# One K tile first, unread products at the start, parameters mid-way: reordering the first stage of a hybrid layer

## The chip, the cores and the metric

The kernel runs on one core of a Trainium2 chip. The metric is the device time of one execution in microseconds (us); less is better. The chip has five engines with queues of their own: PE (TensorE, matrix products), DVE (VectorE), ACT (ScalarE), POOL (GpSimd) and SP (SyncE, which here only issues DMA transfers). Each engine takes its instructions strictly in the order of its queue; between engines they wait on semaphores.

## The reference, cut to what matters

One layer of a streaming encoder for 256 prompt positions and 32 sample positions, 288 columns in all, in fp32:

```python
xn   = rmsnorm(x, norm_mix_pre)
proj = xn @ w_in                 # -> u_pool | z | xs, B, C | dt
pool = pool_mixer(u_pool, ...)
ssd  = ssd_mixer(z, xBC, dt, ...) # causal conv, chunked scan, gate, norm
x    = x + rmsnorm(concat[pool, ssd] @ w_out, norm_mix_post)
x    = x + rmsnorm(ConvFFN(rmsnorm(x, norm_ffn_pre)), norm_ffn_post)
```

D_MODEL is 2048 (16 K tiles of 128 rows). Only the beginning concerns us: the read of x and the product of xn with the columns of w_in for B (256), C (256) and dt (32).

## The kernel before, in words

Activations lie with features on the partitions and the 288 positions along the free axis. Every fp32 product is made of three products in a faster format: the weight block `raw` is split into a high part `whi` (ACT) and a rest `wlo` (DVE), the activation likewise, and PE adds high x high (L162), high x low (L163) and low x high (L164) into one PSUM bank. `project()` does this for a group of output columns over all K tiles; weights are streamed by SP into four `raw` buffers, and `whi` and `wlo` have four buffers each.

The first stage reads x itself. `input_tiles()` issues the transfers of `xt` (two blocks of 128 prompt rows) and `xs_` (32 sample rows), and for each K tile transposes them on PE (L298, L299, L300) into one bank of three that serve small results. From there ACT writes the high half of `xn`, scaled by the gain g (L119), DVE the low half (L120), and DVE a copy `xT` (L303) that is stored to DRAM for the residual (L305). The gain comes from `g_in`, transposed by `columns()` (L280, L281). The normalisation by the root mean square is applied later: ACT squares whole rows of xt and xs_ (L347, L348), PE spreads the result over the partitions (L354, `prs`), and DVE copies it to `rstd` (L358). Each accumulator of the stage is then multiplied by rstd as it is emptied (`conv_in()`, L379 and L380).

The stage is one call of `project()` with three groups, B, C and dt, which accumulate in five banks (all that the accumulators have). The K tiles go in steps of 2, 2, 4, 4, 4, with the next step's tiles asked for ahead of this step's products. dt is 32 columns wide, so `split_narrow()` puts both halves side by side and needs two products (L184, L185). At K tile 12 `parameters()` transposes the small parameters (`columns()` and L324, copied by L281 and L325). After the stage come the xs columns of w_in, 256 at a time, with the same accumulator banks.

POOL sets constants at the start (ident, ones, tri, rec, scan_one, four `ebuf` by L244), and then issues the transfers of the small parameters. DVE derives `sel`, `pick` and `sel64` from ident (L235 to L238). A scheduler orders each engine's queue by priority; what is marked `keep_in_program_order` stays in the order of the source.

Of the kernel before, what the change touches and what calls it, by code (L numbers as in the profile page):

```python
# [35 lines left out]
HALF = NF // 2  # L36
MW = 416
EVAC = 100
XS_RATE = (0, 0, 1, 0, 1, 0, 1, 0)
Z_RATE = (1, 0, 1, 1, 0, 1, 1, 0)  # L40
TAIL = NT - P
# [3 lines left out]
def body(  # L45
# [78 lines left out]

    ahead = [0]

    def fetch_w(view, kb, nk, c0, nc_):
        raw = wpool.tile([P, nk, nc_], F32, tag="raw", name="raw")
        with tc.high_priority(offset=ahead[0]):
            sp.dma_start(out=raw, in_=view[:, kb : kb + nk, c0 : c0 + nc_])  # L130
        return raw

    def split_w(raw, kb, nk, nc_, after=()):

        out = []
        step = min(nk, 1024 // nc_)
        for k in range(0, nk, step):
            n = min(step, nk - k)
            hi = wpool.tile([P, n, nc_], F32R, tag="hi", name="whi")
            lo = wpool.tile([P, n, nc_], F32R, tag="lo", name="wlo")  # L140
            with ExitStack() as order:
                order.enter_context(tc.high_priority(offset=ahead[0]))
                for ins in after:
                    order.enter_context(tc.issue_after(ins.ins))
                act.activation(hi, raw[:, k : k + n, :], AF.Copy)  # L145
                dve.tensor_tensor(lo, raw[:, k : k + n, :], hi.bitcast(F32), op=ALU.subtract)  # L146
            out.append([(kb + k + i, hi[:, i, :], lo[:, i, :]) for i in range(n)])
        return out

    def split_narrow(raw, kb, nk, nc_, after):  # L150

        both = xin.tile([P, nk, 2, nc_], F32R, tag="both", bufs=2, name="both")
        with ExitStack() as order:
            order.enter_context(tc.high_priority(offset=ahead[0]))
            for ins in after:
                order.enter_context(tc.issue_after(ins.ins))
            act.activation(both[:, :, 0, :], raw, AF.Copy)
            dve.tensor_tensor(both[:, :, 1, :], raw, both[:, :, 0, :].bitcast(F32), op=ALU.subtract)
        return [(kb + k, both[:, k, :, :].rearrange("p r c -> p (r c)")) for k in range(nk)]

    def mm3(out, wh, wl, a, start, stop):
# [4 lines left out]
    def project(view, groups, acts, ksplit, before=None, done=None, spare=(), hold=(), behind=None):  # L166


        n_all = sum(-(-w // P) for _, w in groups)
        accs = [acc_ps.tile([P, NT], F32, tag="acc", name="acc") for m in range(n_all - len(spare))]  # L170
        accs.extend(spare)
        k_first, k_last = ksplit[0][0], ksplit[-1][0] + ksplit[-1][1] - 1
        after = before(*ksplit[0]) if before else None
        for i, (kb, n) in enumerate(ksplit):
            raws = [fetch_w(view, kb, n, c0, w) for c0, w in groups]
            nxt = None
            if before and i + 1 < len(ksplit):
                nxt = before(*ksplit[i + 1])
            m0 = 0
            for raw, (c0, w) in zip(raws, groups):  # L180
                if w < P:
                    for k, both in split_narrow(raw, kb, n, w, after or ()):
                        o = accs[m0][: 2 * w, :]
                        pe.matmul(o, both, acts[k][:, 0, :], start=k == k_first, stop=False)  # L184
                        pe.matmul(o, both, acts[k][:, 1, :], start=False, stop=k == k_last)  # L185
                    continue
# [12 lines left out]
            after = nxt  # L199
        return accs  # L200

    def blocks_out(d, t, src, pool_):
# [15 lines left out]
    pool.affine_select(  # L218
        out=tri, in_=ones, pattern=[[1, P]], compare_op=ALU.is_ge, fill=0.0, base=0, channel_multiplier=-1
    )  # L220
    eps_t = const.tile([P, 1], F32, name="eps_t")
    pool.memset(eps_t, EPS)
    warm = const.tile([P, 1], F32, name="warm")
    tc.keep_in_program_order(act.activation(warm, eps_t, AF.Copy))
# [7 lines left out]
    sel = const.tile([HEADS, 2], F32, name="sel")  # L232
    pick = const.tile([HEADS, NX], F32, name="pick")
    id32 = ident[:HEADS, :HEADS]
    dve.tensor_reduce(sel, id32.rearrange("h (t r) -> h r t", r=2), axis=AX.X, op=ALU.add)  # L235
    dve.tensor_reduce(pick, id32.rearrange("h (t r) -> h t r", r=2), axis=AX.X, op=ALU.add)
    sel64 = const.tile([HEADS, 2, 64], F32, name="sel64")
    dve.tensor_copy(sel64, sel.unsqueeze(2).broadcast_to([HEADS, 2, 64]))  # L238

    NE = 4  # L240
    ebuf = []
    for i in range(NE):
        e = const.tile([P, 326], F32, name=f"ebuf{i}")
        pool.memset(e, 0.0)  # L244
        ebuf.append(e)

    start = ExitStack()
    xin = start.enter_context(tc.tile_pool(name="xin", bufs=1))

    g0_in = xin.tile([KD, P], F32, name="g0_in")  # L250
    act.dma_start(out=g0_in, in_=rows(norm_mix_pre))
# [3 lines left out]
    pool.dma_start(out=pb_in[76:92, :], in_=rows(norm_ffn_pre))  # L255
    pool.dma_start(out=pb_in[92:108, :], in_=rows(norm_ffn_post))
    xt = xin.tile([P, 2, D_MODEL], F32, name="xt")
    xs_ = xin.tile([NS, D_MODEL], F32, name="xs_")
    xpv = x_prompt.rearrange("o (b p) d -> p (o b) d", p=P)
    pa_in = xin.tile([124, P], F32, name="pa_in")  # L260
    pool.dma_start(out=pa_in[0:80, :], in_=rows3(ssd_conv_w))
# [15 lines left out]
    def columns(src, n, name):  # L277
        o = const.tile([P, n], F32, name=name)
        p_ = aux([P, n], "pt")
        pe.transpose(p_, src, ident[:n, :n])  # L280
        dve.tensor_copy(o, p_)  # L281
        return o

    g_mix_pre = columns(g0_in, KD, "g0")


# [1 line left out]
    xT = xin.tile([P, KD, NT], F32, name="xT")  # L288
    xT_d = dram.tile([P, KD, NT], F32, name="xT_d")

    def input_tiles(kb, n):
        c = slice(kb * P, (kb + n) * P)
        sp.dma_start(out=xt[:, :, c], in_=xpv[:, :, c])
        sp.dma_start(out=xs_[:, c], in_=x_sample[0][:, c])
        for t in range(kb, kb + n):
            p_ = aux([P, NT], "pt")
            c = slice(t * P, (t + 1) * P)
            pe.transpose(p_[:, 0:P], xt[:, 0, c], ident)  # L298
            pe.transpose(p_[:, P:NP_], xt[:, 1, c], ident)  # L299
            pe.transpose(p_[:, NP_:NT], xs_[:, c], ident[:NS, :NS])  # L300
            a = atile("xn")
            last = split_from(a, p_, g_mix_pre[:, t : t + 1])
            dve.tensor_copy(xT[:, t, :], p_)  # L303
            xn.append(a)
        act.dma_start(out=xT_d[:, kb : kb + n, :], in_=xT[:, kb : kb + n, :])  # L305
        return last

    def parameters():
        pb = columns(pb_in, 108, "pb")
# [18 lines left out]
    prm = []  # L328

    def first_in(kb, n):  # L330
        if kb == 12:
            prm.extend(parameters())
        return input_tiles(kb, n)

    win = w_in.rearrange("o (k p) c -> p (o k) c", p=P)
    O_Z, O_X = D_POOL, D_POOL + D_SSD
    O_B, O_C, O_DT = O_X + D_SSD, O_X + D_SSD + 256, O_X + CONV
    first = project(
        win, [(O_B, 256), (O_C, 256), (O_DT, HEADS)], xn, [(0, 2), (2, 2), (4, 4), (8, 4), (12, 4)], first_in
    )  # L340

    ahead[0] = 200
    ssum = xin.tile([P, 3], F32, name="ssum")
    pool.memset(ssum, 1.0)
    junk = xin.tile([P, D_MODEL], F32, name="junk")
    for b in range(2):
        act.activation(junk, xt[:, b, :], AF.Square, accum_out=ssum[:, b : b + 1])  # L347
    act.activation(junk[:NS, :], xs_, AF.Square, accum_out=ssum[:NS, 2:3])  # L348
    rs = xin.tile([P, 3], F32, name="rs")
    act.activation(rs, ssum, AF.Sqrt, bias=eps_t, scale=1.0 / D_MODEL)  # L350
    dve.reciprocal(rs, rs)
    p_ = aux([P, NT], "prs")
    for b, (o, n) in enumerate(BLK):
        pe.matmul(  # L354
            p_[:, o : o + n], rs[:n, b : b + 1].broadcast_to([n, P]), ident[:n, :n], start=True, stop=True
        )
    rstd = const.tile([P, NT], F32, tag="spread", bufs=3, name="rstd")
    dve.tensor_copy(rstd, p_)  # L358

# [784 lines left out]
```

## Time and profile before

| | |
|---|---|
| median of three runs | 1360.85 us (1360.6, 1360.85, 1362.29) |
| the profiled execution | 1361.99 us; span in the trace 1360.2 us |
| mean granted clock of PE | 0.995 |
| PE busy | 1340.6 us, 99% of the span |
| DVE, ACT, POOL busy | 879.0, 666.9, 234.3 us |
| DMA | 252.13 MB, mean 185 GB/s |

Times in a trace count from the start of the span. The span is what the profiler saw of the engines; the execution's own time holds 1.8 us more that lie around it. Busy time of PE counts a matrix product until its modelled end, so neighbouring products overlap, and a stretch in which PE counts as busy may still run at a lower rate: the distance from one start to the next tells that.

### The profile page before, as it was taken

Reading aid. Unit: us, or ns where it says so; the run is one execution under the profiler, and the core shown is the slowest. Engines: PE = TensorE matmul, PEld = TensorE weight load, DVE = VectorE, ACT = ScalarE, POOL = GpSimd, SP = SyncE. Lnnn points to the kernel's source line nnn. Section 1 sums busy time; section 2 is a strip of 40 time slices with the busy share of each in tenths; the row PEclk is TensorE's granted clock in tenths of the full one; section 3 lists DMA queues with packets and bytes.
Section 4 is the critical chain, followed back from the end, with each engine's and each line's share of the span. In section 5 each row is a group of like instructions: output and inputs, shape, how many; then the busy total and the mean of one; then the engine's idle time right before and its main releaser. Section 6 shows DMA issues by size and latency. Waiting matters only on the chain.

```text
span 1360.2 us, 25798 instructions
## 1 busy us (share of the span) xinstructions
PE 1340.6 (99%) x10231; PEld 1330.2 (98%) x10231; DVE 879.0 (65%) x1515; ACT 666.9 (49%) x1000; POOL 234.3 (17%) x394
## 2 busy tenths in 40 slices
PE   8999999999999999999999999999999999999996
PEld 7999999999999999999999999999999999999995
DVE  6898988679544468977666644335666666654443
ACT  6557757446434455654444433334444444454441
POOL 3132112132224310211121100001111111101110
PEclk9999999999999999999999999999999999999998
DMA  9869995465656536766554545554544545577662
GB/s 267 248 188 284 261 261 162 138 215 172 217 183 209 170 109 196 228 185 191 177 164 156 172 148 169 171 178 155 179 162 157 182 158 161 173 224 198 181 174 87
DMA packets 300135, 252.13 MB, mean 185 GB/s; under 512 B 75728, under 2 KB 293050, under 8 KB 299886
## 3 DMA queue, kind: packets, MB, share of 16 engines
q1 hardware_dynamic: 296810, 243.20, 58.6%
q0 software_dynamic: 2320, 4.65, 1.2%
q10 hardware_dynamic: 884, 2.63, 0.5%
q8 instruction: 80, 1.31, 0.4%
q14 instruction: 41, 0.34, 0.1%
HBM read 236.13 MB, written 14.31 MB: 184 GB/s over the span
## 4 chain that ended last, share of the span: by engine, by line
PE 97%; DMA 1%; DVE 1%; ACT 0%; issue 0%; DVEq 0%; ACTq 0%
PE acc L162 31%; PE acc L164 31%; PE acc L163 31%; PE pst L842 1%; PE py L561 1%; DMA raw<-in_w_up 1%; DVE xr L1102 0%; DVE wlo L146 0%; PE py L563 0%; DMA xt<-in_x_prompt 0%; PE pt L298 0%; ACT whi L145 0%; PE pt L300 0%; PE acc_x L162 0%; PE acc_x L163 0%
## 5 line engine op out<-in xcount | busy, mean ns | idle before, releaser
L146 DVE TENSOR_TENSOR wlo<-raw,whi 128x1024 fp32r<-128x1024 f32 (+1 forms) x416 | 494.0, 1189 | 365.2 <-ACT whi L145 359.3
L145 ACT ACTIVATE whi<-raw 128x1024 fp32r<-128x1024 f32 (+1 forms) x416 | 427.2, 1028 | 513.4 <-PE acc L163 436.9
L162 PE MATMUL acc<-hn,whi 128*128 128x288 f32 x1376 | 404.8, 296 | 0.6 <-DVE ebuf L943 0.6
L163 PE MATMUL acc<-hn,whi 128*128 128x288 f32 x1376 | 403.6, 294 | 0.0
L164 PE MATMUL acc<-hn,wlo 128*128 128x288 f32 x1376 | 403.4, 294 | 0.0
L164 PEld LDWEIGHTS acc<-hn,wlo 128*128 128x128 f32 x1376 | 260.0, 189 | 0.0
L163 PEld LDWEIGHTS acc<-hn,whi 128*128 128x128 f32 x1376 | 260.0, 189 | 0.0
L162 PEld LDWEIGHTS acc<-hn,whi 128*128 128x128 f32 x1376 | 257.5, 188 | 0.8 <-PE acc_x L164 0.8
L162 PE MATMUL acc<-xn,whi 128*128 128x288 f32 x704 | 209.5, 299 | 0.0
L162 PE MATMUL acc<-fa,whi 128*128 128x288 f32 x704 | 208.7, 296 | 0.0
L163 PE MATMUL acc<-fa,whi 128*128 128x288 f32 x704 | 208.6, 296 | 0.0
L163 PE MATMUL acc<-xn,whi 128*128 128x288 f32 x704 | 208.3, 297 | 0.0
L164 PE MATMUL acc<-fa,wlo 128*128 128x288 f32 x704 | 208.2, 296 | 0.0
L164 PE MATMUL acc<-xn,wlo 128*128 128x288 f32 x704 | 207.6, 297 | 0.0
L163 PEld LDWEIGHTS acc<-xn,whi 128*128 128x128 f32 x704 | 134.0, 191 | 0.2
L164 PEld LDWEIGHTS acc<-xn,wlo 128*128 128x128 f32 x704 | 133.3, 190 | 0.3
L162 PEld LDWEIGHTS acc<-xn,whi 128*128 128x128 f32 x704 | 132.7, 189 | 0.4
L163 PEld LDWEIGHTS acc<-fa,whi 128*128 128x128 f32 x704 | 133.0, 189 | 0.0
L162 PEld LDWEIGHTS acc<-fa,whi 128*128 128x128 f32 x704 | 132.4, 188 | 0.0
L164 PEld LDWEIGHTS acc<-fa,wlo 128*128 128x128 f32 x704 | 132.2, 188 | 0.0
L944 POOL COPY fc_stage<-ebuf 128x4 f32<-128x4 f32 x88 | 27.0, 307 | 511.8 <-DVE ebuf L943 466.6
L950 DVE SCALAR_TENSOR_TENSOR fc<-ebuf,pf,fc 128x290 f32<-128x290 f32 x176 | 90.1, 516 | 3.0 <-ACT fc L948 0.3
(317 smaller groups left out, 1622.2 us busy)
## 6 DMA issues: line engine op xcount, KB each, us to landing
raw<-in_w_up SPq DMA_DIRECT2D x80, 1024.0 KB, 5.2
raw<-in_w_in SPq DMA_DIRECT2D x40, 1024.0 KB, 5.8
raw<-in_w_down SPq DMA_DIRECT2D x32, 1024.0 KB, 5.3
raw<-in_w_out SPq DMA_DIRECT2D x24, 1024.0 KB, 6.4
raw<-in_w_down SPq DMA_DIRECT2D x16, 768.0 KB, 4.6
raw<-in_w_up SPq DMA_DIRECT2D x14, 512.0 KB, 4.2
gb<-g_d SPq DMA_DIRECT2D x8, 832.0 KB, 4.8
raw<-in_w_in SPq DMA_DIRECT2D x6, 512.0 KB, 6.4
```

The source lines that it names most:

```text
L145: act.activation(hi, raw[:, k : k + n, :], AF.Copy)
L146: dve.tensor_tensor(lo, raw[:, k : k + n, :], hi.bitcast(F32), op=ALU.subtract)
L162: pe.matmul(out, wh, a[:, 0, :], start=start, stop=False)
L163: pe.matmul(out, wh, a[:, 1, :], start=False, stop=False)
L164: pe.matmul(out, wl, a[:, 0, :], start=False, stop=stop)
L561: ins = pe.matmul(y[c, 0:256], xw[:, 0, f_], m[:, h, 0:256], start=True, stop=False)
L842: ins = pe.matmul(st[:, o, :], x_, btok[:, gi, b, :], start=b != 1, stop=b != 0)
L944: pool.tensor_copy(fc_stage[:, :, :, i], e[:, 256:324].rearrange("p (s c) -> p s c", c=34)[:, :, 0:2])
L950: dve.scalar_tensor_tensor(c, e[:, r_ : r_ + 290], pf[:, r_, i : i + 1], c, op0=ALU.mult, op1=ALU.add)
```

## The change

The first stage is written out in place of the call of `project()`:

- K tiles come in steps of 1, 1, 1, 1, 2, 2, 2, 3, 3 (`FIRST`). For each, SP issues the transfer of xt and then one of the weights of B, C and dt together, 544 columns; three steps are issued ahead. The first 256 columns of xs_ come by ACT's queue, the rest by one transfer of SP's, after the second step. xT is stored in three transfers (`STORES`).
- PE runs products that nobody reads (`keep_busy()`): seven ahead of the transpose of g, five after tile 0's transposes. Their operand `busy` is filled by three DVE copies from `ones`.
- For K tile 0, the products high x high and high x low of all four blocks stand ahead of tile 1's transposes, and low x high behind them. From then on a step's products follow the transposes of the next step.
- xs_ is now 128 rows high with zeros in the first 96 (DVE and POOL set them), so that its transpose (L309) is a full product with ident's last 32 columns; the three products that spread rstd (L425) have 128 rows likewise.
- `parameters()` comes with step 6 (`PARAMETERS`), that is K tile 8, and no longer with K tile 12.
- sel, pick and sel64 are made after the stage.

The diff, cut to its core:

```diff
+FIRST = ((0, 1), (1, 1), (2, 1), (3, 1), (4, 2), (6, 2), (8, 2), (10, 3), (13, 3))
+STORES = {3: 0, 9: 4, 15: 10}
+BUSY = (7, 5)
+PARAMETERS = 6
...
+    busy = xin.tile([P, NT], F32R, name="busy")
+    for o, n in BLK:
+        tc.keep_in_program_order(dve.tensor_copy(busy[:, o : o + n], ones[:, 0:n]))
+
+    xs_ = xin.tile([P, D_MODEL], F32, name="xs_")
+    tc.keep_in_program_order(dve.memset(xs_[: P - NS, : 2 * P], 0.0))
...
+    pool.memset(xs_[: P - NS, 2 * P :], 0.0)
     NE = 4
     ebuf = []
...
-    xs_ = xin.tile([NS, D_MODEL], F32, name="xs_")
+    tc.keep_in_program_order(act.dma_start(out=xs_[P - NS :, : 2 * P], in_=x_sample[0][:, : 2 * P]))
+    tc.keep_in_program_order(act.activation(warm, eps_t, AF.Copy))
+    busy_ps = aux([P, NT], "busy_ps")
+
+    def keep_busy(n):
+
+        for _ in range(n):
+            tc.keep_in_program_order(pe.matmul(busy_ps, busy[:, 0:P], busy, start=True, stop=True))
...
+    keep_busy(BUSY[0])
     g_mix_pre = columns(g0_in, KD, "g0")
...
+    def input_tile(t):
+        p_ = aux([P, NT], "pt")
+        c = slice(t * P, (t + 1) * P)
+        pin = tc.keep_in_program_order if t < 4 else lambda ins: ins
+        pin(pe.transpose(p_[:, 0:P], xt[:, 0, c], ident))
+        pin(pe.transpose(p_[:, P:NP_], xt[:, 1, c], ident))
+        pin(pe.matmul(p_[:, NP_:NT], xs_[:, c], ident[:, P - NS :], start=True, stop=True))
...
+        def split():
+            pin(act.activation(a[:, 0, :], p_, AF.Copy, scale=g_mix_pre[:, t : t + 1]))
+            pin(dve.scalar_tensor_tensor(
+                a[:, 1, :], p_, g_mix_pre[:, t : t + 1], a[:, 0, :].bitcast(F32), op0=ALU.mult, op1=ALU.subtract
+            ))
+
+        def keep():
+            pin(dve.tensor_copy(xT[:, t, :], p_))
+            if t in STORES:
+                c = slice(STORES[t], t + 1)
+                act.dma_start(out=xT_d[:, c, :], in_=xT[:, c, :])
...
-    first = project(
-        win, [(O_B, 256), (O_C, 256), (O_DT, HEADS)], xn, [(0, 2), (2, 2), (4, 4), (8, 4), (12, 4)], first_in
-    )
+    first = [acc_ps.tile([P, NT], F32, tag="acc", name="acc") for _ in range(5)]
+    raws = {}
+
+    def first_load(i):
+        if i < len(FIRST):
+            kb, n = FIRST[i]
+            input_load(kb, n)
+            raws[i] = fetch_w(win, kb, n, O_B, NB + HEADS, pin=True)
+
+    for i in range(3):
+        if i == 2:
+            c = slice(2 * P, D_MODEL)
+            tc.keep_in_program_order(sp.dma_start(out=xs_[P - NS :, c], in_=x_sample[0][:, c]))
+        first_load(i)
+    def first_tiles(i):
+        if i == PARAMETERS:
+            prm.extend(parameters())
+        return [input_tile(t) for t in range(FIRST[i][0], sum(FIRST[i]))] if i < len(FIRST) else []
+
+    prm = []
+    steps = first_tiles(0)
+    keep_busy(BUSY[1])
+    for i, (kb, n) in enumerate(FIRST):
+        first_load(i + 3)
+        pin = i < 4
+        ahead_steps = first_tiles(i + 1) if i else []
+        for split, _ in steps:
+            split()
+        raw = raws.pop(i)
+        parts = split_w(raw[:, :, :NB], kb, n, NB, pin=pin)
+        for _, keep in steps:
+            keep()
+        narrow = split_narrow(raw[:, :, NB:], kb, n, HEADS, pin)
+        if not i:
+            (_, hi, lo), = parts.pop()
+            for w, r in ((hi, 0), (hi, 1), (lo, 0)):
+                if w is lo:
+                    ahead_steps = first_tiles(1)
+                for m in range(4):
+                    tc.keep_in_program_order(pe.matmul(
+                        first[m], w[:, m * P : (m + 1) * P], xn[0][:, r, :], start=w is hi and not r, stop=False
+                    ))
+        for part in parts:
+            for m in range(4):
+                c = slice(m * P, (m + 1) * P)
+                for k, hi, lo in part:
+                    mm3(first[m], hi[:, c], lo[:, c], xn[k], k == 0, k == KD - 1)
+        for k, both in narrow:
+            o = first[4][: 2 * HEADS, :]
+            pe.matmul(o, both, xn[k][:, 0, :], start=k == 0, stop=False)
+            pe.matmul(o, both, xn[k][:, 1, :], start=False, stop=k == KD - 1)
+        steps = ahead_steps
 
     ahead[0] = 200
+    sel = const.tile([HEADS, 2], F32, name="sel")
...
+    dve.tensor_copy(sel64, sel.unsqueeze(2).broadcast_to([HEADS, 2, 64]))
...
-        pe.matmul(
-            p_[:, o : o + n], rs[:n, b : b + 1].broadcast_to([n, P]), ident[:n, :n], start=True, stop=True
-        )
+        pe.matmul(p_[:, o : o + n], rs[:, b : b + 1].broadcast_to([P, P]), ident[:, P - n :], start=True, stop=True)
```

In the changed kernel the lines of the same statements have other numbers: the three products of a step are L170, L171 and L172 (for K tile 0 L392), the transposes L307 to L309, xn L314 and L315, xT L320, the splits L152 and L153, the parameter copies L288 and L344, the copies into busy L227, the unread products L264, rstd L427, and the accumulators are emptied by L448 and L449. In DVE's queue the rstd copy is followed by an instruction of the mixer (`hv`, L539), a split of weights (L153) and then L448 and L449.

More of the change, by code (lines that the diff above doesn't have):

```diff
@@ L125, in body, with fetch_w, split_w @@
     ahead = [0]
-    def fetch_w(view, kb, nk, c0, nc_):
+    def fetch_w(view, kb, nk, c0, nc_, pin=False):
         raw = wpool.tile([P, nk, nc_], F32, tag="raw", name="raw")
         with tc.high_priority(offset=ahead[0]):
-            sp.dma_start(out=raw, in_=view[:, kb : kb + nk, c0 : c0 + nc_])
+            ins = sp.dma_start(out=raw, in_=view[:, kb : kb + nk, c0 : c0 + nc_])
+            if pin:
+                tc.keep_in_program_order(ins)
         return raw
-    def split_w(raw, kb, nk, nc_, after=()):
+    def split_w(raw, kb, nk, nc_, after=(), pin=False):
         out = []
@@ L144, in split_w, with split_narrow @@
                     order.enter_context(tc.issue_after(ins.ins))
-                act.activation(hi, raw[:, k : k + n, :], AF.Copy)
-                dve.tensor_tensor(lo, raw[:, k : k + n, :], hi.bitcast(F32), op=ALU.subtract)
+                parts = (
+                    act.activation(hi, raw[:, k : k + n, :], AF.Copy),
+                    dve.tensor_tensor(lo, raw[:, k : k + n, :], hi.bitcast(F32), op=ALU.subtract),
+                )
+                if pin:
+                    for ins in parts:
+                        tc.keep_in_program_order(ins)
             out.append([(kb + k + i, hi[:, i, :], lo[:, i, :]) for i in range(n)])
         return out
-    def split_narrow(raw, kb, nk, nc_, after):
+    def split_narrow(raw, kb, nk, nc_, pin):
+        pin = tc.keep_in_program_order if pin else lambda ins: ins
         both = xin.tile([P, nk, 2, nc_], F32R, tag="both", bufs=2, name="both")
[L153 to L158, printed above, removed]
+        pin(act.activation(both[:, :, 0, :], raw, AF.Copy))
+        pin(dve.tensor_tensor(both[:, :, 1, :], raw, both[:, :, 0, :].bitcast(F32), op=ALU.subtract))
         return [(kb + k, both[:, k, :, :].rearrange("p r c -> p (r c)")) for k in range(nk)]
@@ L180, in project @@
             for raw, (c0, w) in zip(raws, groups):
[L181 to L186, printed above, removed]
                 parts = split_w(raw, kb, n, w, ((after or ()) if m0 else ()) + (hold if i else ()))
@@ L220, in body @@
     )
+    start = ExitStack()
+    xin = start.enter_context(tc.tile_pool(name="xin", bufs=1))
+    busy = xin.tile([P, NT], F32R, name="busy")
[3 more added lines that the diff above has]
+    tc.keep_in_program_order(dve.memset(xs_[: P - NS, : 2 * P], 0.0))
     eps_t = const.tile([P, 1], F32, name="eps_t")
@@ L223, in body @@
     warm = const.tile([P, 1], F32, name="warm")
-    tc.keep_in_program_order(act.activation(warm, eps_t, AF.Copy))
     rec = const.tile([P, 16], F32, name="rec")
@@ L231, in body @@
         pool.memset(scan_one[:, c : c + 1], 0.0)
[L232 to L238, printed above, removed]
+    pool.memset(xs_[: P - NS, 2 * P :], 0.0)
     NE = 4
@@ L245, in body @@
         ebuf.append(e)
-    start = ExitStack()
-    xin = start.enter_context(tc.tile_pool(name="xin", bufs=1))
     g0_in = xin.tile([KD, P], F32, name="g0_in")
@@ L289, in body, with input_load @@
     xT_d = dram.tile([P, KD, NT], F32, name="xT_d")
-    def input_tiles(kb, n):
+    def input_load(kb, n):
         c = slice(kb * P, (kb + n) * P)
[L293 to L306, printed above, removed]
+        tc.keep_in_program_order(sp.dma_start(out=xt[:, :, c], in_=xpv[:, :, c]))
+    def input_tile(t):
[5 more added lines that the diff above has]
+        pin(pe.matmul(p_[:, NP_:NT], xs_[:, c], ident[:, P - NS :], start=True, stop=True))
+        a = atile("xn")
+        xn.append(a)
+        def split():
[8 more added lines that the diff above has]
+                act.dma_start(out=xT_d[:, c, :], in_=xT[:, c, :])
+        return split, keep
     def parameters():
@@ L326, in parameters @@
         return pb, pah, g_mix_post, g_ffn_pre, g_ffn_post, pa, p_scale, g_ssd, pc, pf
[L328 to L333, printed above, removed]
     win = w_in.rearrange("o (k p) c -> p (o k) c", p=P)
     O_Z, O_X = D_POOL, D_POOL + D_SSD
-    O_B, O_C, O_DT = O_X + D_SSD, O_X + D_SSD + 256, O_X + CONV
-    first = project(
-        win, [(O_B, 256), (O_C, 256), (O_DT, HEADS)], xn, [(0, 2), (2, 2), (4, 4), (8, 4), (12, 4)], first_in
-    )
@@ L342, in body @@
-    ahead[0] = 200
+    O_B = O_X + D_SSD
+    NB = 512
+    first = [acc_ps.tile([P, NT], F32, tag="acc", name="acc") for _ in range(5)]
[10 more added lines that the diff above has]
+        first_load(i)
@@ new lines, in body @@
+    ahead[0] = 200
+    sel = const.tile([HEADS, 2], F32, name="sel")
+    pick = const.tile([HEADS, NX], F32, name="pick")
+    id32 = ident[:HEADS, :HEADS]
+    tc.keep_in_program_order(dve.tensor_reduce(sel, id32.rearrange("h (t r) -> h r t", r=2), axis=AX.X, op=ALU.add))
+    tc.keep_in_program_order(dve.tensor_reduce(pick, id32.rearrange("h (t r) -> h t r", r=2), axis=AX.X, op=ALU.add))
+    sel64 = const.tile([HEADS, 2, 64], F32, name="sel64")
+    dve.tensor_copy(sel64, sel.unsqueeze(2).broadcast_to([HEADS, 2, 64]))
@@ L347, in body @@
         act.activation(junk, xt[:, b, :], AF.Square, accum_out=ssum[:, b : b + 1])
-    act.activation(junk[:NS, :], xs_, AF.Square, accum_out=ssum[:NS, 2:3])
+    act.activation(junk[P - NS :, :], xs_[P - NS :, :], AF.Square, accum_out=ssum[P - NS :, 2:3])
     rs = xin.tile([P, 3], F32, name="rs")
```

## The prediction

> **What bounds the kernel now.** I read the page first: the busy shares and the chain that ended last.
>
> ```profile
> PE 1340.6 (99%) x10231; PEld 1330.2 (98%) x10231; DVE 879.0 (65%) x1515; ACT 666.9 (49%) x1000; POOL 234.3 (17%) x394
> PE 97%; DMA 1%; DVE 1%; ACT 0%; issue 0%; DVEq 0%; ACTq 0%
> ```
>
> TensorE (PE) is busy 99% of the span and carries 97% of the chain. Nothing that runs beside it matters until PE has to wait; what PE loses at the start stays lost, because no later stretch has slack. So I look for the places where PE does less than it can. The table of windows counts its instructions per stretch (columns: length, then busy time and count for each engine, clock, DMA share, GB/s).
>
> ```profile
> 0.00:7.00 7.00, 1.85 (x8) 1.33 (x9) 3.47 (x7) 2.89 (x5) 6.36 (x41) 1.00 0.67 186
> 7.00:10.00 3.00, 3.00 (x13) 2.59 (x14) 2.27 (x6) 1.57 (x4) 2.19 (x5) 1.00 0.97 289
> 10.00:13.00 3.00, 3.00 (x15) 2.98 (x14) 2.10 (x5) 0.72 (x2) 1.27 (x4) 1.00 1.01 340
> ...
> 25.00:30.00 5.00, 5.00 (x36) 4.75 (x37) 3.53 (x8) 5.00 (x8) 0.00 (x0) 1.00 0.78 206
> ...
> 1000.00:1020.00 20.00, 20.00 (x153) 20.00 (x152) 14.08 (x25) 9.69 (x14) 4.37 (x7) 1.00 0.48 158
> ```
>
> In steady work PE does 153 in 20 us, 0.131 each. From 7 to 13 us it does 28 in 6 us, 0.21 to 0.24 each, although it counts as busy: starts in the timeline are 0.24 apart until 13.15 and 0.13 after. So the clock in fact opens at about 13.1. The timeline shows what stands before that.
>
> ```profile
> 1.80 2.08 DVE L238 COPY sel<-sel 32x128 f32<-32x128 f32 x1
> 2.52 1.28 POOL L244 MEMSET ebuf<- 128x326 f32 x4
> 3.67 0.26 PE L280 MATMUL pt<-ident,g_in 16*128 16x16 f32 x1 [3.67 <-DMA g_in<-in_norm_mix_pre]
> 3.75 0.69 POOL L253 DMA_DIRECT2D pb_in<-in_state_ssd_conv  x1
> 4.07 0.48 PE L298 MATMUL pt<-ident,xt 128*128 128x128 f32 x1
> 5.46 0.50 ACT L119 ACTIVATE xn<-pt,g 128x288 fp32r<-128x288 f32 x1 [2.66 <-PE pt L300]
> 5.86 0.62 ACT L145 ACTIVATE whi<-raw 128x512 fp32r<-128x512 f32 x1
> 6.87 0.45 PE L298 MATMUL pt<-ident,xt 128*128 128x128 f32 x1 [1.34 <-DVE xT L303]
> 7.19 0.83 PE L162 MATMUL acc<-xn,whi 128*128 128x288 f32 x2
> ```
>
> PE waits 3.67 us for g_in, transposes, waits 1.34 more, and starts its first product at 7.19. The last place is the end of the first stage, in VectorE's (DVE's) timeline.
>
> ```profile
> 43.17 0.46 DVE L358 COPY rstd<-prs 128x288 f32<-128x288 f32 x1
> 43.55 2.35 DVE L146 TENSOR_TENSOR wlo<-raw,whi 128x1024 fp32r<-128x1024 f32 x2
> 45.82 0.42 DVE L379 TENSOR_TENSOR ebuf<-acc,rstd 128x256 f32<-128x256 f32 x1
> 46.15 0.18 DVE L380 TENSOR_TENSOR ebuf<-acc,rstd 128x32 f32<-128x32 f32 x1
> ```
>
> The copies L379/L380 empty the accumulators for the next projection. B's accumulators are finished early there, as B, C and dt are three groups, and PE still has C and dt products to run meanwhile: no PE wait appears.
>
> **The change, part by part** (less PE time is minus).
>
> *Start of the products.* Now the first xt transfer holds one K tile, not two. Tile 0's three transposes follow 4.07 by 0.26 + 0.22 + about 0.42 (the spacing and length of the rows at half rate), to about 5.0; xn 0.50 and then whi 0.62 on ScalarE (ACT) give about 6.2. Against 7.19: **-1.0**. The 12 unread products (7 before g's transpose, 5 after tile 0) stand in PE time that is idle now: 7 x 0.24 = 1.7 us before 3.67, 5 x 0.24 = 1.2 us between 5.0 and 6.2. So 0, if they start on time; they wait for three DVE copies out of ones.
>
> *Clock.* Those 28 instructions would take 28 x 0.131 = 3.7 us at the steady pace and took 6: 2.3 lost. After, from 6.2 on at half rate until the clock opens. Seen once, it opened about 6 us after the first product, with waits in between. The unread products begin at about 1.6 instead, so I put the opening at 8.6 (half way between 13.1 and 4.1, where 1.6 + the 2.5 us of unread work would end): 2.4 x (1 - 0.131/0.24) = 1.1 lost. Net **-1.2**; -2.3 if open by 6.2, +0.8 if it opens at 13.1 again (6.9 x 0.45 = 3.1 lost).
>
> The Trainium skill, "TensorE: Matmul & The Clock Gate", Part 1, says that the rate doubles after a busy window of about 3.4 us, and that this window runs free of the kernel's start; by it the opening could lie anywhere from about 5 to 8.5, a little better than my 8.6, and the trace's one opening can't decide it.
>
> *Tile transposes.* L300 (32 rows of weights) becomes L309 (128 rows, the first 96 zero).
>
> ```profile
> PEld pt L300 <- issue: 2.7, 14, 0.3
> ```
>
> The weight load before L300 stood 2.7 us without cause shown, 14 times: 0.19 each, and PE hides a part. With half of it gained, 16 x 0.08 = -1.3, and the six prs matmuls (0.78 on the chain, 0.13 each) become two-pass ones of 128 rows, ~0.6: -0.2, but L309's second operand pass is as long as before. I take **-1.2** together; bounds 0 and -2.8.
>
> *Loads.* One raw of 544 columns in place of three, three steps ahead, SP 565 DMAs to 559; xs's rest goes once, behind raw 1, its first 256 columns on ACT's queue ahead of the table load (1.28 us, done at 2.6 now; about 0.5 later, and xn starts only at 5). The 20-25 us windows show DMA saturated at 335 GB/s; 9 MB of input need 27 us at that rate against 40 us of PE work, so 0. xT goes out in three stores. POOL zeroes 96x1792 of xs_ before ebuf: 1792/326 x 0.32 = 1.75 us, which moves all its parameter DMAs later; the last (issued 14.16, landing 6.5 later, 20.7) comes at 22.5, before its transposes at about 25: 0.
>
> *Parameters mid-way.* Their copies pc and pf on DVE stand behind splits wlo (1.22) that wait for raw blocks, and the tile transposes need their PSUM banks; ACT's squares (1.92 each, L347) stand between xn's. PE's cover is one tile's products, 14 x 0.131 = 1.8. One of each exposed would be 1.22 + 1.92 = 3.1, none 0; 25-30 us already shows ACT at 5.00 of 5. Half: **+1.5**.
>
> *The end of the first stage: a new wait.* All five accumulators now end together. On PE, the last products, two prs matmuls, then the first xs product, which needs accumulator 0 emptied (L448, L449). DVE's queue ahead of that: rstd copy (waits prs), hv (also waits for the last xT store), the split wlo 1.22, L448, L448, L449. The ACT half of that split waits for a buffer that PE frees only seven instructions before the stage's end. So from PE's end: rstd 0.46, hv 0.1, wlo 1.13 (at pace), 0.33 + 0.33 + 0.18 = 2.53, with PE holding nothing else in its queue: **+2.6**. Bounds: 0 if rstd and the split are done in time, 3.7 if the store lands 1.1 late (xT stores take 2.8 to 6.6 to land). Behind it are queued all later splits, but xs weights for eight K tiles are then ready.
>
> *Sum:* -1.0 - 1.2 - 1.2 + 1.5 + 2.6 = +0.7. The profiled execution took 1361.99, with a span of 1360.2 and 1.8 around it; +0.7 gives 1362.7. It stands 1.14 above the median of 1360.85, so the median becomes about **1361.6**.
>
> **Rivals.** *(a) The unread products are late: slower.* L238, a copy inside SBUF of 32x128, took 2.08 us and ended at 3.88, just after POOL's unbroken memsets ended at 3.80; L235 and L236 beside them took 0.17. The three copies out of ones (L227) are of the same kind and would become ready at 1.20, when POOL is in its chain, which will end at 3.80 + 1.65 = about 5.45. The unread products, in PE's queue ahead of everything, then start at 5.6; 7 x 0.24, g, tile 0 and five more put the first product at 9.6, +3.4; the clock saves 0.5 and loads that are further ahead 0.5 of it back: +2.4 on top, net +3.1, **1364.0**, up to +4.1 (1365). Against: POOL is idle between 1.23 and 1.26, and a copy that gets in there goes through, with the others close behind. It decides whether the copies end before 3.7.
>
> The Trainium skill, "SBUF — State Buffer", "two separate sides", says that this port pair is an exclusive lock that whichever of DVE's two-port copy and POOL starts first holds for its whole instruction; L238's 2.08 us agrees, and by the rule either order can come out here.
>
> *(b) The last wait is not there and the clock opens by 6.2: faster.* If rstd's copy and the split come before the last products, the sum is -1.0 - 2.3 - 1.2 + 1.5 = -3.0, **1357.9**; without the mid-way stall -4.5, 1356.4. For it: DVE is only 65% busy and before shows no wait here. Against: the order of its queue.
>
> *(c) The clock gains nothing* because transposes break up the work: +2.0 more, net +2.7, **1363.6**.
>
> **Numbers.** Forecast 0.42, (a) 0.30, (b) 0.20, (c) 0.08. About 0.2% (2.7 us) is what a measurement of this kernel can tell from no change: 1358.1 to 1363.6. Of the forecast's case 0.24 is inside, 0.08 faster, 0.10 slower, as its bounds are wide; of (a) 0.25 is slower, 0.05 inside; of (b) 0.17 faster, 0.03 inside; (c) splits evenly. Faster 0.25, same 0.36, slower 0.39. The range leaves out about a tenth at each end: from 1356.8, near the better form of (b), to 1366.2, which is (a)'s upper end and about 1.2 for the spread of the three runs (1360.6 to 1362.29). The forecast's own is 1358.6 to 1364.2.
>
> **What would show it.** First product (L392) near 6.2, or 9.6 with L227's copies ending after POOL's memsets: (a). Starts 0.13 apart from about 8.6. PE waits of about 2.6 us on DVE L449 before the first xs product (L170, 45 to 50 us); none there means (b). Waits at 25 to 32 us on xn L315 or pf L344. Before 50 us all of it; a difference later would prove me wrong, since PE's order is then the same work.

## The result, and the profile after

The changed kernel is slower: 1375.36 us median (1373.77 to 1377.09) against 1360.99 for the kernel before in the same comparison, a ratio of 1.0103 (95% interval 1.0091 to 1.0115). That is 14.4 us, where 0.7 us were forecast, and outside the range. The profiled execution took 1376.30, its span 1374.6; the profiled one of before took 1361.99.

PE's share of the chain that ended last was 97% before. From the page of after:

```profile
PE 1346.3 (98%) x10259; PEld 1336.6 (97%) x10259; DVE 879.4 (64%) x1524; ACT 666.5 (48%) x1005; POOL 233.1 (17%) x395
PE 90%; DMA 5%; DVE 3%; SPq 1%; ACT 1%; issue 1%; DVEq 0%; POOL 0%; ACTq 0%; POOLq 0%
```

DMA and DVE now hold 8% of the chain, and so the end was not set by the beginning alone. The waits of PE (us in total, times, longest) say where:

```profile
PE acc L172 <- DVE wlo L153: 5.4, 6, 2.0
PE acc L170 <- DVE ebuf L449: 3.0, 1, 3.0
PE busy_ps L264 <- DVE busy L227: 1.8, 1, 1.8
PE pt L307 <- DVE pc L288: 1.8, 1, 1.8
PE py L630 <- DVE m L618: 1.8, 1, 1.8
```

The line on L264 is the wait at the very start, which the kernel before has too (3.67 us, for g_in). The others are new: 2.2 us at the parameters (L307: the 1.8 for pc, and 0.4 more for pf), 3.0 at the end of the first stage (L449), and 7.2 (5.4 + 1.8) between 128 and 218 us, in the mixer (the stage that follows, with the scan of `ssd_mixer`), where the change edits nothing and PE never waited before. Two windows of the mixer, of the kernel before and then of the changed one:

```profile
120.00:140.00 20.00, 20.00 (x183) 18.82 (x182) 18.32 (x34) 20.00 (x45) 2.56 (x4) 1.00 0.95 279
...
200.00:220.00 20.00, 20.00 (x186) 19.01 (x185) 15.16 (x24) 12.42 (x26) 5.98 (x5) 1.00 0.57 160
```

```profile
120.00:140.00 20.00, 18.24 (x172) 17.18 (x171) 16.76 (x29) 19.31 (x40) 0.80 (x3) 1.00 0.85 242
...
200.00:220.00 20.00, 17.52 (x144) 16.55 (x145) 15.32 (x24) 9.54 (x16) 3.36 (x4) 1.00 0.77 210
```

PE was busy all the time there before, and is idle for 1.8 and 2.5 of these 20 us now. A second loss stands in the first 60 us: behind the waits at the parameters and at the stage's end, the granted clock fell back to half for one stretch of 3.41 us each (the rows are shown further down). Behind the mixer's waits, the longest of 2.0 us, it did not fall.

The start went much as planned. From the timeline of after:

```profile
1.20 0.54 DVE L227 CAST busy<-ones 128x128 fp32r<-128x128 f32 x3 [1.20 <-POOL rec L236]
1.79 2.05 PE L264 MATMUL busy_ps<-busy 128*128 128x288 f32 x7 [1.79 <-DVE busy L227]
...
6.40 0.80 PE L392 MATMUL acc<-xn,whi 128*128 128x288 f32 x2
```

The first product begins at 6.40 (7.19 before), the clock opens at 9.9 (13.2), and a tile's transposes cost 0.44 us at full clock, with the delay of the product behind them (0.59 before).

**The account, at one place.** The first of the products psum_t, behind which PE's order is the same in both kernels, begins at 230.8 before and 245.2 after: all 14.4 us are lost by then. Waits: 2.2 + 3.0 + 7.2 = 12.4. Two half-rate stretches: 3.41 x (1 - 0.131/0.24) = 1.55 each, 3.1. Ten stops, each of which costs about 0.16 beyond its listed wait, as the last product counts as busy for 0.29 where the next would follow at 0.13: 1.6. That makes 17.1, so the start gave back about 2.7; this figure is what is left over, and not a measurement of its own.

### The profile page after: what moved, and what is told of

It reads as the page before. It is cut to its first block, busy times and chain, and to the rows that moved or that the text cites. A ratio compares the mean times of both kernels' runs of the same rounds, so it can differ in the third digit from the quotient of the medians.

```text
span 1374.6 us, 25841 instructions
## 1 busy us (share of the span) xinstructions
PE 1346.3 (98%) x10259; PEld 1336.6 (97%) x10259; DVE 879.4 (64%) x1524; ACT 666.5 (48%) x1005; POOL 233.1 (17%) x395
## 4 chain that ended last, share of the span: by engine, by line
PE 90%; DMA 5%; DVE 3%; SPq 1%; ACT 1%; issue 1%; DVEq 0%; POOL 0%; ACTq 0%; POOLq 0%
PE acc L170 29%; PE acc L172 29%; PE acc L171 28%; DMA xs_d<-blocks 2%; SPq L210 1%; DVE wlo L153 1%; PE pst L911 1%; DMA gb<-g_d 1%; DMA xk<-xs_d 1%; DMA xt<-in_x_prompt 1%; DMA raw<-in_w_in 0%; DVE xr L1171 0%; PE py L630 0%; DVE m L618 0%; DVE conv L461 0%
## 5 line engine op out<-in xcount | busy, mean ns | idle before, releaser
L153 DVE TENSOR_TENSOR wlo<-raw,whi 128x1024 fp32r<-128x1024 f32 (+1 forms) x417 | 493.6, 1186 | 360.2 <-ACT whi L152 349.7
L152 ACT ACTIVATE whi<-raw 128x1024 fp32r<-128x1024 f32 (+1 forms) x417 | 426.7, 1026 | 498.0 <-PE acc L171 417.5
L170 PE MATMUL acc<-hn,whi 128*128 128x288 f32 x1376 | 404.3, 295 | 0.3 <-DVE ebuf L1012 0.3
L171 PE MATMUL acc<-hn,whi 128*128 128x288 f32 x1376 | 403.3, 294 | 0.0
L172 PE MATMUL acc<-hn,wlo 128*128 128x288 f32 x1376 | 403.0, 294 | 0.0
L171 PEld LDWEIGHTS acc<-hn,whi 128*128 128x128 f32 x1376 | 259.8, 189 | 0.0
L172 PEld LDWEIGHTS acc<-hn,wlo 128*128 128x128 f32 x1376 | 259.6, 189 | 0.0
L170 PEld LDWEIGHTS acc<-hn,whi 128*128 128x128 f32 x1376 | 257.4, 187 | 0.5 <-PE acc_x L172 0.5
L172 PE MATMUL acc<-xn,wlo 128*128 128x288 f32 x700 | 205.9, 297 | 5.4 <-DVE wlo L153 5.4
L170 PE MATMUL acc<-fa,whi 128*128 128x288 f32 x704 | 208.6, 296 | 0.0
L171 PE MATMUL acc<-fa,whi 128*128 128x288 f32 x704 | 208.4, 296 | 0.0
L172 PE MATMUL acc<-fa,wlo 128*128 128x288 f32 x704 | 208.0, 295 | 0.0
L170 PE MATMUL acc<-xn,whi 128*128 128x288 f32 x700 | 204.1, 299 | 3.1 <-DVE ebuf L449 3.0
L171 PE MATMUL acc<-xn,whi 128*128 128x288 f32 x700 | 206.1, 297 | 0.0
L172 PEld LDWEIGHTS acc<-xn,wlo 128*128 128x128 f32 x700 | 132.6, 190 | 7.0 <-DVE wlo L153 6.8
L170 PEld LDWEIGHTS acc<-xn,whi 128*128 128x128 f32 x700 | 130.4, 189 | 3.6 <-issue 3.0
L171 PEld LDWEIGHTS acc<-xn,whi 128*128 128x128 f32 x700 | 132.9, 191 | 0.0
L171 PEld LDWEIGHTS acc<-fa,whi 128*128 128x128 f32 x704 | 132.7, 188 | 0.0
L170 PEld LDWEIGHTS acc<-fa,whi 128*128 128x128 f32 x704 | 132.3, 188 | 0.0
L172 PEld LDWEIGHTS acc<-fa,wlo 128*128 128x128 f32 x704 | 132.0, 188 | 0.0
```

What stands on the lines that cost most here:

```text
L152: act.activation(hi, raw[:, k : k + n, :], AF.Copy),
L170: pe.matmul(out, wh, a[:, 0, :], start=start, stop=False)
L171: pe.matmul(out, wh, a[:, 1, :], start=False, stop=False)
L172: pe.matmul(out, wl, a[:, 0, :], start=False, stop=stop)
```

## The experiments

Two theories were put against each other for the mixer. A: the queues of the mixer were given another order, and in that order DVE waits for the mixer's trips through DRAM. B: the accumulators are emptied late at the stage's end, and the mixer never catches up.

**e1, the parameters two steps later.**

```diff
-PARAMETERS = 6
+PARAMETERS = 8
```

> The changed kernel with the parameters two steps later (PARAMETERS 8 in place of 6). In the program, the copies pc and pf then stand later in DVE's queue, and the rstd copy stands directly ahead of L448 and L449, with no split between. All theories: no PE wait at 26 to 30 us (2.1 us) and no half-rate stretch behind it (1.5); no 3.0 us wait at the stage's end and no half-rate stretch behind it (1.5): 8.1 us less in the first 60 us. Theory A (the waits at 120 to 220 us, 7.2 us, come from the order that the queues of the mixer were given): this kernel has another order again, so these waits change without a rule, 0 to 10 us. Theory B (they come from the late emptying of the accumulators): they go too, and the time is near 1375.4 - 8.1 - 7.2 = 1360.

Measured 1361.88 (1359.68 to 1366.1), ratio 1.0008 (0.9996 to 1.002); the profiled execution took 1363.71. In it the wait at the stage's end is gone, 1.2 us are left at the parameters with one half-rate stretch (41.5 to 45.0), and 1.7 in the mixer. Both theories had room for that; the parameters' place cost far more than their own wait, since it also decided the order of DVE's queue 20 us later.

**e2, the stage's end alone.**

```diff
-    for b, (o, n) in enumerate(BLK):
-        pe.matmul(p_[:, o : o + n], rs[:, b : b + 1].broadcast_to([P, P]), ident[:, P - n :], start=True, stop=True)
     rstd = const.tile([P, NT], F32, tag="spread", bufs=3, name="rstd")
-    dve.tensor_copy(rstd, p_)
+    with tc.high_priority(offset=400):
+        for b, (o, n) in enumerate(BLK):
+            pe.matmul(p_[:, o : o + n], rs[:, b : b + 1].broadcast_to([P, P]), ident[:, P - n :], start=True, stop=True)
+        dve.tensor_copy(rstd, p_)
```

> The changed kernel with the three prs products and the rstd copy given a high priority, nothing else. In the program, rstd's copy then stands ahead of the last splits and L448/L449 follow it. The 3.0 us wait at the stage's end and the 1.5 us of half rate behind it go; the waits at 26 to 30 us stay. Theory A: the waits at 120 to 220 us are another number, 0 to 10. Theory B: gone, near 1375.4 - 4.5 - 7.2 = 1363.7.

Measured 1364.17, ratio 1.0017 (1.0003 to 1.003): 11 us of the 14 are gone. The 3.0 us wait and its half-rate stretch went as expected; the wait at the parameters (2.4) and its half rate stayed; the mixer's waits fell from 7.2 to 1.9. Again both theories fit.

**e3 and e4, small edits of the kernel before**: the unread products alone, and the parameters at K tile 8.

```diff
+    busy = xin.tile([P, NT], F32R, name="busy")
+    for o, n in BLK:
+        tc.keep_in_program_order(dve.tensor_copy(busy[:, o : o + n], ones[:, 0:n]))
...
+    keep_busy(7)
     g_mix_pre = columns(g0_in, KD, "g0")
...
+        if kb == 0:
+            keep_busy(5)
```

> The kernel before with the 12 unread products alone (7 ahead of g's transpose, 5 behind the first two tiles' transposes). The clock opens 3.4 us earlier than 13.1, at about 9.8, which is worth 1.5 us. Theory A: the queues of the mixer are in another order than before here too, so there are PE waits at 100 to 220 us and the kernel gets slower although its start is better: 1361 to 1367. Theory B: no waits there, 1359.5.

```diff
-        if kb == 12:
+        if kb == 8:
```

> The kernel before with the parameters one step earlier (K tile 8 in place of 12), which leaves the start as it is and gives the mixer's queues another order. Theory A: PE waits of 1 to 8 us at 100 to 220 us, 1362 to 1369. Theory B: at most a wait of 2 us where the parameters stand, and none later: 1361 to 1363.

e3 measured 1368.06, ratio 1.0057 (1.0037 to 1.0077): slower than either theory said, with the clock open at 10.2, near the expected 9.8, 1.6 us of waits before 60 us and 3.1 in the mixer, although its accumulators are not emptied late. e4 measured 1364.26, ratio 1.0019 (1.0006 to 1.0033), with no wait in the mixer at all, so A in its first form (any new order costs) fell; what it lost was lost at the parameters, with a half-rate stretch at 33.2 to 36.7. Both lie above what B allowed, and e3 has waits in the mixer without a late end. I then sharpened A: an order costs what it makes DVE wait for the mixer's DRAM trips, beyond what DVE has to spare.

**e5, the order without the end.** This one tells the two apart: the stage's end stays as it is in the changed kernel.

```diff
-    def blocks_out(d, t, src, pool_):
+    def blocks_out(d, t, src, pool_, bufs=1):
...
-        s = pool_.tile([P, NT], F32, tag="blocks", bufs=1, name="blocks")
+        s = pool_.tile([P, NT], F32, tag="blocks", bufs=bufs, name="blocks")
...
-        blocks_out(b_d, gi, bc[gi], mp)
+        blocks_out(b_d, gi, bc[gi], mp, 2)
...
-            blocks_out(xs_d, 2 * i + j, o, mp)
+            blocks_out(xs_d, 2 * i + j, o, mp, 2)
```

> The changed kernel with two buffers in place of one for the blocks that the mixer writes to DRAM (the copy waits for the store of the block before it). The first stage's queues are the same, with the waits at 26 to 30 us and the 3.0 us at the stage's end: those and their half-rate stretches stay, 8.1 us. The mixer's queues are in another order. Theory A, sharpened by the first four runs (PE's waits at 100 to 230 us follow DVE's own waits for the mixer's round trips through DRAM: 13 us of DVE waits gave 0 us on PE before, 23.6 gave 7.2 after, 9 to 18 gave 0 to 2.9): DVE's waits for xs_d's blocks (12.1 us) go in most part, PE's waits there fall to 0 to 3 us, 1368 to 1371. Theory B (the late end): it is still there, so PE's 7 us stay, 1375.

Measured 1366.33 (1364.57 to 1366.92), ratio 1.0035 (1.0019 to 1.0051), 9 us less than the changed kernel and below the 1368 to 1371 that A gave. PE's waits in e5:

```profile
PE acc L170 <- DVE ebuf L449: 3.0, 1, 3.0
...
PE pt L307 <- DVE pc L288: 1.5, 1, 1.5
...
```

The late end is there to the tenth, with both half-rate stretches, and the mixer's lines are gone; DVE's waits for xs_d's blocks, 12.1 us in the changed kernel, are gone too. B falls as the cause by itself. That the late end adds to DVE's delay in the changed kernel's own order is not excluded, as no run has that order without the late end.

**e9, its control**: the same two buffers in the kernel before.

> Control of e5: the kernel before with two buffers for the mixer's blocks. PE has no waits in the mixer there, so nothing is to be gained: 1360.5 to 1362 if the new order of the queues costs nothing either, up to 1364 if it does. If two buffers are worth something of their own beside the change (that is, e5's 9 us are not the change's 7.2 us come back), it gets faster by several us.

Measured 1366.88, ratio 1.0041 (1.0025 to 1.0057): 5.4 us slower, where at most 3 were expected. The edit that saved 9 us in one kernel costs 5 in the other, so its worth is not in the second buffer by itself. PE's waits in e9, and below them DVE's between 46 and 230 us:

```profile
PE acc L164 <- DVE wlo L146: 3.5, 1, 3.5
...
PE py L561 <- DVE m L549: 1.1, 1, 1.1
```

```profile
DVE xw L538 <- DMA xk<-xs_d: 12.5, 3, 4.4
```

The first stage has no wait beyond those of the kernel before (1.6 us for xt where that one has 1.3). All of DVE's waits for DRAM are three for a reload of xs (`xk`). PE's two waits in the mixer, 1.1 and 3.5 us, come 2.8 and 4.8 us behind the first and the third; the second, 4.4 us long, cost PE nothing. One half-rate stretch (197.9 to 201.3) follows the longer wait. The mechanism, in the changed kernel, in the timelines of SP and of DVE:

```profile
122.78 0.38 SPq L603 DMA_DIRECT2D xk<-xs_d  x1
```

```profile
127.46 0.96 DVE L607 TENSOR_TENSOR xw<-xk,tok 128x768 f32<-128x768 f32 x1 [1.78 <-DMA xk<-xs_d]
128.34 1.88 DVE L618 TENSOR_TENSOR m<-m,cbt 128x1664 f32<-128x1664 f32 x1
```

xs goes to DRAM and comes back as `xk`; 4.7 us after the reload was issued xw can run, and DVE's queue had only 2.9 us of other work to put between. It stood for 1.78 us, `m` came late, and the product that needs m (py, L630, at 130.27) waited 1.76. In the kernel before the same reload, the second of eight, is issued at 118.13, and its xw runs at 123.98 with no wait, as DVE's queue has more work between:

```profile
118.13 0.62 SPq L534 DMA_DIRECT2D xk<-xs_d  x1
```

```profile
123.98 0.92 DVE L538 TENSOR_TENSOR xw<-xk,tok 128x768 f32<-128x768 f32 x1
```

This is shown instruction by instruction for part of the 7.2 us. Three of PE's seven waits in the mixer (at 130.27, 171.07 and 217.86, together 3.2 us) stand within 3 us of a DVE wait for a trip. Ahead of the other four (at 152.06, 174.89, 201.57 and 205.31, together 4.0 us) DVE had worked without a pause for 6 to 13 us: there the split comes late because the queue ahead of it is full, and that an earlier trip put the queue behind is argued, not shown.

Over all kernels, DVE's waits for these trips (blocks, xk, h) between 46 and 230 us against PE's waits between 60 and 240: e5 6.0 and 0, e10 6.4 and 0, e11 6.9 and 0, e12 7.9 and 0, e7 8.2 and 0, e4 9.1 and 0, before 13.0 and 0, e1 12.3 and 1.7, e6 12.4 and 1.4, e9 12.5 and 4.6, e2 15.0 and 1.9, e8 16.3 and 2.7, e3 18.0 and 3.1, after 23.6 and 7.2. Up to 9.1 us PE paid nothing; from 12.3 to 13.0 it paid between nothing (before) and 4.6 (e9); from 15.0 on it always paid. So the sum ranks the kernels roughly, and is no price: 1.4 of e6's and 0.7 of e1's PE waits are not at a split or a product of the mixer but on its norm (`rg`, L669, at 236 to 238 us).

**e6, the kernel of e1 again, and e7, e1 without the unread products**. The edit is that of e7 against e1.

```diff
-BUSY = (7, 5)
+BUSY = (0, 0)
```

> The same kernel as e1 once more, for the spread of its clock: opening between 5 and 10 us, a half-rate stretch if a wait at 38 to 42 us falls into one window with under about 1.9 of 3.41 us busy; 1359.7 to 1364.

> e1 (parameters two steps later) without the 12 unread products. The first real product comes at the same 6.4 us or up to 0.3 earlier; the clock opens at 13 to 14 us in place of 7.4 (e1) to 9.9: 1.6 to 2.5 us slower up to 14 us. Its mixer's queues may differ, so the comparison is made up to 20 us in the trace. If the unread products do nothing, the opening is within 1 us of e1's.

e6 gave 1361.84 in one run, its clock open at 10.2, where e1's opened at 7.4; it has only 0.2 us of wait at the parameters and no half-rate stretch. e7 measured 1362.15 (ratio 1.001, 0.9998 to 1.0021), its clock open at 11.9, earlier than the expected 13 to 14. The transposes of tile 7, whose place in PE's order is the same in the three, begin at 18.68 in e1, 19.95 in e6 and 20.85 in e7. So the unread products bring 0.9 to 2.2 us there, as expected or somewhat less; at the end, the medians of e1 and e7 differ by 0.3 us, within the spread, and do not measure it, as e7 has no wait in the mixer where e1 has 1.7.

**e8, the parameters one step later and all small copies early** (PARAMETERS 7; the edit of e2; a high priority for L288 and L344).

> A version that may beat both: the changed kernel with the parameters one step later (7), their copies, the prs products and the rstd copy at a high priority. No wait at the stage's end; where the parameters' copies stand behind a split whose block lands late, a wait of 1 to 2 us and one half-rate stretch of 3.4 us (1.5 us) remain, without it 0. Mixer waits 0 to 3. 1357 to 1362.

Measured 1363.97, ratio 1.0018 (1.0007 to 1.0029): above what was expected. The wait moved: 2.6 us on xn behind a square on ACT, 0.8 at the parameters, a half-rate stretch, and 2.7 in the mixer.

**e10, both repairs** (e2 and e5 together), and **e11, e12, the version that was to beat both** (e1 and e5 together; e12 is e11 timed again).

> The changed kernel with both: the high priority for the prs products and the rstd copy (e2), and two blocks buffers (e5). What is left is the wait at 26 to 30 us (1.9) and its half-rate stretch (1.5). By the sum of the trace (start, clock and transposes bring 2.7): 1361.2 - 2.7 + 3.4 = 1361.9, if the mixer's order is harmless.

> The changed kernel with the parameters two steps later (e1) and two blocks buffers (e5): no wait at the stage's end, a small one at the parameters (0.2 to 1.2, with a half-rate stretch in some executions), none in the mixer. By the sum: 1361.2 - 2.7 + 0.8 (small waits) + 0.5 = 1359.8, faster than both kernels; 1361 to 1363 if the mixer's new order costs.

> The kernel of e11 once more, timed in more rounds, to settle whether it beats the kernel before: e11 gave a ratio of 0.9994 with an interval that reaches 1.0003. By the trace of e11 (the first 60 us: small waits of 1.9 us in all, no half-rate stretch, none in the mixer) it should stay 0.5 to 1 us faster: ratio 0.9992 to 0.9997.

e10 measured 1362.41, ratio 1.001 (0.9999 to 1.002), no wait in the mixer or at the stage's end, 1.4 us of small waits before 30 us and a half-rate stretch behind the parameters: the account of the trace said 1361.9. e11 measured 1360.72, 0.9 above its sum, ratio 0.9994 (0.9984 to 1.0003), and e12 1360.62, ratio 0.9992 (0.9983 to 1.0001). Both point to 0.7 to 1 us faster than the kernel before, and neither interval leaves out no change. It is 14.7 us faster than the changed kernel.

## Why the prediction was wrong

*The start (forecast -3.4 for products, clock and transposes).* Near in size, in part by luck: the account leaves 2.7 at psum_t. First product 6.40 for 6.2; clock at 9.9 for 8.6 (7.4 to 10.6 over the kernels that have the unread products, 11.9 to 13.6 over the four without); the transposes were mis-sized, -1.2 with prs, where 16 x (0.59 - 0.44) = 2.4 is what the rows give. Taken singly the rows give more than the account: 0.8 for the first product, 3.3 x 0.45 = 1.5 for the clock and 2.4, together 4.7. The first term left something out that goes the other way: when its first product began, the kernel before had already put tiles 0 and 1 and the prompt rows of tile 2 through their transposes, in time that it waited anyway, and the changed kernel tile 0 alone. The changed kernel runs those later, in about 1 us (tile 1 from 8.44 to 9.15, tile 2 from 10.36 to 10.71). The other 1 us is not accounted for. (The 12 unread products at 0.24 are 2.9 us, not the 2.5 in the working; the opening would have become 8.8.)

*Parameters mid-way (+1.5).* The mechanism was the one named, pc behind a split whose block had not landed: 2.2 us listed, about 0.7 above the term.

*The end of the stage (+2.6).* The named queue (rstd, hv, a split, L448, L448, L449) shows instruction by instruction, with 3.0 us:

```profile
50.14 0.46 DVE L427 COPY rstd<-prs 128x288 f32<-128x288 f32 x1 [0.18 <-PE prs L425]
50.80 0.31 DVE L539 TENSOR_SCALAR hv<-pick,hp 32x16 f32<-32x16 f32 x1 [0.21 <-DVE rstd L427]
50.95 1.21 DVE L153 TENSOR_TENSOR wlo<-raw,whi 128x1024 fp32r<-128x1024 f32 x1
52.08 0.74 DVE L448 TENSOR_TENSOR ebuf<-acc,rstd 128x256 f32<-128x256 f32 x2
52.75 0.17 DVE L449 TENSOR_TENSOR ebuf<-acc,rstd 128x32 f32<-128x32 f32 x1
```

*What the sum left out, first: the clock falls again* (3.1 us). I priced the waits as waits only. In these traces the clock changes in steps of 3.41 us: the two half-rate stretches of the changed kernel begin 6 and 13 such steps behind the opening at 9.9, and last one step each. A step that a wait empties by more than half was followed by one at half rate. The windows of the changed kernel on those very stretches:

```profile
26.99:30.40 3.41, 1.49 (x11) 1.21 (x12) 2.81 (x6) 3.41 (x8) 0.00 (x0) 0.99 1.07 374
30.40:33.81 3.41, 3.41 (x15) 3.38 (x16) 2.50 (x5) 3.41 (x5) 0.00 (x0) 0.51 1.09 348
50.88:54.29 3.41, 1.23 (x9) 1.26 (x10) 3.40 (x12) 2.15 (x4) 0.93 (x5) 0.99 0.60 127
54.29:57.70 3.41, 3.41 (x16) 3.41 (x15) 3.38 (x9) 0.00 (x0) 0.00 (x0) 0.51 1.17 329
...
197.65:201.06 3.41, 1.88 (x15) 1.65 (x13) 3.41 (x9) 3.41 (x6) 0.24 (x2) 1.00 1.09 329
```

PE was busy for 1.49 and 1.23 us of 3.41, and the next stretch ran at half; at 197.65, busy for 1.88, it did not. The Trainium skill, "TensorE: Matmul & The Clock Gate", Part 1, gives the fall back after at least one idle window of about 3.4 us, and its section "Why this matters for your kernels" warns of idle gaps above about 3 us; here gaps of 1.8 and 3.0 us, in windows that were never idle as a whole, were enough.

*Second, and most: the mixer* (7.2 us of waits, about 8 with the stops). The step that failed is the sentence "a difference later would prove me wrong, since PE's order is then the same work". The sum has no term for the time behind the first stage. The work there was the same, but its order was not: the scheduler had dealt the queues anew. In the traces PE runs the same sequence in both kernels only from 166 us on (before; 177 after), and DVE from 211 (227). The order stands in the two programs and could be compared ahead of any run. I took PE's lack of waits there in the kernel before for slack. It was an order that hid the DRAM trips: 13.0 us of DVE waits for them there cost PE nothing. How much of the 7.2 us each wait of DVE's makes stays open, as said at e9.

*Rivals.* (a) did not happen: the three copies from ones ran at 1.20 in 0.54 us, beside a POOL instruction. They change the type, and the trace calls them CAST; L238, a plain COPY, takes 0.20 where it now stands (L413, at 40 us, with POOL idle) and took 2.08 beside POOL's memsets. That shows that L238 was held, and not that a cast would be. The copies also began at 1.20, at the short gap in POOL's work that the prediction names, so whether the gap or the type let them through is open. (b) did not come about: the last wait was there. (c), that the clock gains nothing, is contradicted by 9.9 against 13.2, and by e7. The opening itself moved by 2.8 us between two executions of one kernel, though (e1 and e6).

## What to carry to other kernels

Where a scheduler orders the queues, an edit at the start is also an edit of all that the scheduler places after it: compare the order of every engine up to where the two programs agree again, and price the waits of that stretch too, above all reloads from DRAM that stand close ahead of their use. A wait of PE has a second price, a stretch at half clock, if it empties more than half of one of the clock's windows of 3.41 us; so two short waits in different windows can cost less than one long one (e11's four in the first 45 us, 1.9 us in two windows, brought no such stretch). And that the bound engine never waits does not say that there is slack: with 13.0 us of DVE waits for DRAM PE paid nothing in the kernel before, and with 12.5 it paid 4.6 us in e9.

## What was not expected of the hardware

- Between the clock's opening and 1340 us every fall lasted exactly one window of 3.41 us, and began a whole number of such windows behind the opening (6 to 54 of them, in ten falls). With the windows laid there, those that hold products alone part cleanly: PE busy for 0.78 (e9), 0.92 (e5) and 1.2 us (after) was followed by a fall; 1.75 and 1.84 (e3), 1.79 (e8), 1.9 and 2.1 (after) was not. Windows that hold transposes too do not: 0.83 (e8), 1.5 (after), 1.55 (e2), 1.60 (e5), 1.82 (e1), 2.33 (e10) and 2.57 (e4) were followed by a fall, 2.11 (e12), 2.40 (e7) and 2.48 (e11) were not. That transposes count for less would fit the falls at 2.33 and 2.57, but e12's window holds twelve transposes and five products and was followed by none; what counts there is open.
- The windows stand at another place in each execution (openings at 7.4 and 10.2 us for the same kernel, e1 and e6), so the same wait is followed by a fall in one execution and not in the next: 1.2 us at the parameters was in e1, 1.3 us in e12 was not. That is part of the spread of 2.4 to 6.4 us that these kernels show from run to run, where the kernel before has 1.7 to 2.8: of e1's eight executions the three with a mean granted clock of 0.994 took 1363.7 to 1366.1 us, the five with 0.995 or 0.996 took 1359.7 to 1362.0. One half-rate stretch is 1.55 us, so it is not all of the spread.
